# Seven half-size products of block sums in place of eight, on part of the FFN down projection of a hybrid encoder block

## The chip, the cores and the metric

The kernel runs on one core of one Trainium2 chip. The metric is the device time of one execution in microseconds (us), lower is better. TensorE (PE) does the matmuls, and its queue of weight loads is shown as PEld; VectorE (DVE), ScalarE (ACT) and GpSimd (POOL) do elementwise work; SyncE (SP) issues the DMAs of the weights.

## The reference, cut to what matters

The reference is one layer of an encoder block on 512 tokens of 1024 features: three token mixers, a gated merge, an output projection, and then a gated convolutional FFN with 2816 hidden features. Only the FFN matters here:

```python
def conv_glu_ffn(h, w_up, w_conv, b_conv, w_down):
    a, u = jnp.split(h @ w_up, 2, axis=-1)
    return (jax.nn.gelu(dwconv3(a, w_conv, b_conv)) * u) @ w_down

x = x + merged @ w_out[l]
x = x + conv_glu_ffn(rms_norm(x, ffn_norm_g[l]), w_ffn_up[l], w_ffn_conv[l], b_ffn_conv[l], w_ffn_down[l])
return rms_norm(x, final_norm_g)
```

Everything is float32. The down projection, the last product, has 2816 x 1024 weights and is applied to 512 tokens.

## The kernel before, in words

**Layout.** Activations lie transposed, features on the 128 partitions and the 512 tokens along the free axis, so that 1024 features are 8 tiles of 128 x 512 and the 2816 hidden features are 22 tiles. A matmul takes a 128 x 128 block of weights as the stationary operand and 512 tokens as the moving one, and adds into a PSUM tile of 128 x 512.

**Precision.** A float32 product is made of three matmuls in the fp32r format (`mm3`, L181 to L184): high part of the weights by high part of the activations, high by low, low by high. The high part is a copy rounded to fp32r on ACT, the low part a subtraction on DVE. Activations are split by `split_act` (L186 to L189) into the tiles named u; weights by `emit_split`, copy `wh` on ACT (L164) and subtraction `wl` on DVE (L165).

**Weights.** All weights lie in DRAM as one flat array of blocks in the order in which they are used (`block_list`, L51 to L79). A block is at most 1024 columns of 128 partitions, 512 KB, that is eight 128 x 128 blocks. `emit_raw` (L135 to L145) issues its DMA on SP (L144) into a ring of three raw buffers `wr`; `emit_split` splits it in one or two halves of up to 512 columns into rings of four `wh` and four `wl` buffers. `weights(key)` (L170 to L179) is called where a product begins: it issues the raw blocks up to three ahead and the splits up to one ahead of that product's block. So the DMA of a block stands in the program well before its use, and waits until the last reader of its raw buffer, a subtraction L165, is done.

**The order of the work.** The program is written as one sequence; a scheduler gives each engine its instructions and adds the semaphore waits. Each engine then runs its own queue strictly in order. Buffers come from rings (scratch tiles `s` of 512 columns, PSUM tiles `mm` and `at`, four each), and a ring's buffer is taken again once its last reader is done.

**The FFN** (L977 to L1032) runs twice, for `hh` = 0 and 1, each time over half of the hidden features, 11 tiles, in two stages.

- Up stage (L981 to L1010): for each of the 11 tiles two projections `ua` and `uu` of 24 matmuls of 512 columns each; on the first the convolution over tokens (`conv`, L308 to L317: DVE, ACT, DVE, DVE), gelu by Tanh (L1002 to L1005, ACT and DVE), a scaling on POOL (L1006); then the product with the second (L1009, DVE), and the split of the result into `UH[j]` and `UL[j]` (`split_act` at L1010).
- Down stage (L1011 to L1032): for each of the 8 feature tiles f, 11 contraction tiles of three matmuls of 512 columns into one PSUM tile (33 matmuls), then one DVE add into `x2[f]` (L1020). The weights of a feature tile are two blocks, of 8 and of 3 contraction tiles. In the second half each tile of x2 is squared on ACT (L1027 for f = 0, L1030), the square is added into `acc3` on POOL (L1031), and x2 is scaled on ACT (L1032). The last feature tile of the second half runs as two passes of 256 tokens, with the final norm and the stores (`finish_a`, `finish_b`, L917 to L975) between and behind them.

`_layout` (from L1040) builds the flat weight array on the host.

Of the kernel before, what the change touches and what calls it, by code (L numbers as in the profile page):

```python
# [50 lines left out]
def block_list():  # L51
# [20 lines left out]
    for hh in range(2):  # L72
        for f in range(HF * hh, HF * (hh + 1)):
            L.append((("ua", f), 1024))
            L.append((("uu", f), 1024))
        for f in range(8):
            for i, n in ((0, 8), (1, 3)):
                L.append((("dn", hh, f, i), n * 128))
    return L  # L79

# [8 lines left out]
BCOLS = {n: (lambda k: P) for n in ("mlk", "o", "xaq", "memk", "naq", "nak", "g", "out", "ua", "uu", "dn")}  # L89
# [6 lines left out]
def hybrid_block(ctx, tc, xT, memT, wflat, vecs, gbias, nabias, outa, outb):  # L96
# [34 lines left out]
    raws, split = {}, {}  # L131
    RAW_AHEAD, SPLIT_AHEAD = 3, 1
    st = {"raw": 0, "split": 0}

    def emit_raw(i):  # L135
        key, n = BLOCKS[i]
        _, off, _ = BINDEX[key]
        r = wp.tile([P, BW], F32, tag="raw", name=nm("wr"), bufs=3)
# [8 lines left out]
    def halves(i):  # L147
        n, c = BLOCKS[i][1], BCOLS[BLOCKS[i][0][0]](BLOCKS[i][0])
        k = n // c
        k0 = k if n <= HWD else (k + 1) // 2  # L150
        return c, [(0, k0)] + ([(k0, k)] if k0 < k else [])

    def emit_split(i):
        key, n = BLOCKS[i]
        r = raws.pop(i)
        c, hs = halves(i)
        split[i] = []
        for a, b in hs:
            h = wp.tile([P, HWD], F32R, tag="hi", name=nm("wh"), bufs=4)
            l = wp.tile([P, HWD], F32R, tag="lo", name=nm("wl"), bufs=4)  # L160
            m = (b - a) * c
            for u, v in ((0, P), (P, m)) if i == 0 and a == 0 else ((0, m),):
                src = r[:, a * c + u:a * c + v]
                A.activation(h[:, u:v], src, AF.Copy)  # L164
                V.tensor_tensor(l[:, u:v], src, h[:, u:v].bitcast(F32), op=ALU.subtract)  # L165
            for k in range(a, b):
                q = slice((k - a) * c, (k - a + 1) * c)
                split[i].append((h[:, q], l[:, q]))

    def weights(key):  # L170
# [37 lines left out]
    SY.dma_start(vec, vecs)  # L208
    emit_raw(0)
# [98 lines left out]
    def conv(ps, rbt, w, b, i, n):  # L308
# [4 lines left out]
        t1 = scr()  # L313
# [662 lines left out]

    for hh in range(2):  # L977
        gu = [unit(F32R) for _ in range(6)]
        UH = [gu[k // 4][:, (k % 4) * S:(k % 4 + 1) * S] for k in range(HF)]
        UL = [gu[3 + k // 4][:, (k % 4) * S:(k % 4 + 1) * S] for k in range(HF)]  # L980
        for j in range(HF):  # L981
# [18 lines left out]
            c = conv(pa, rb2, "ffw", "ffb", f, FT)  # L1000
# [9 lines left out]
            split_act(UH[j], UL[j], c, 0.5)  # L1010
        for f in range(KT):  # L1011
            ws = weights(("dn", hh, f, 0)) + weights(("dn", hh, f, 1))
            last = hh == 1 and f == KT - 1
            for a, b in ((0, 256), (256, 512)) if last else ((0, 512),):
                ps = mmps()[:, :b - a]
                for k in range(HF):
                    mm3(ps, ws[k][0], ws[k][1], UH[k][:, a:b], UL[k][:, a:b], k == 0, k == HF - 1)
                    if last and a > 0 and k == 7:
                        rb3 = row_a(dg3)
# [3 lines left out]
                elif last:  # L1023
                    finish_b(rb3)
# [111 lines left out]
```

## Time and profile before

| what | value |
|---|---|
| time, median of 3 executions | 921.71 us (920.74 to 921.77) |
| the profiled execution's own time | 921.14 us |
| its span, first to last instruction | 919.4 us |
| mean granted TensorE clock | 0.998 of full speed |
| DMA over the span | 96.39 MB, mean 105 GB/s |

The profile is of one execution on the one core. Each engine's busy time is also given as a share of the span. A row of the timeline has the start in us from the span's start, the duration in us, the engine, the line of the kernel, the operation, the tiles written and read with their shapes, and in square brackets how long the engine had been idle and which instruction released it. A row of a group has the shape, the count, the busy time in us and the mean duration of one in ns, and then the idle time before them with what ended most of it. Matmuls are pipelined: one of 512 columns is listed with some 390 ns although the next one starts earlier, so the pace of PE is read from the distance of starts, not from durations.

### The profile page before, as it was taken

To read this page: it belongs to the slowest core of one execution; us is meant where nothing else is said; L and a number is where in the kernel's file an instruction comes from. 1 tells how busy PE (TensorE), PEld (TensorE's weight loads), DVE (VectorE), ACT (ScalarE), POOL (GpSimd) and SP (SyncE) were. 2 spreads that over 40 slices of the span, in tenths; PEclk is the share of its full clock that TensorE was granted. 3 is DMA by queue.
4 is the path that set the end of the run, shared out by engine and by line. 5 is a ranking of instruction groups with operands and counts; after the bars stand their busy time and mean duration, and the time that the engine had idled before them with its cause. 6 is when DMAs were issued, how large, how long until landed. Compare 5 with 4: busy or idle time off the path is not lost.

```text
span 919.4 us, 12132 instructions
## 1 busy us (share of the span) xinstructions
PE 903.8 (98%) x4459; PEld 754.8 (82%) x4459; DVE 576.4 (63%) x979; ACT 437.1 (48%) x875; POOL 134.2 (15%) x155
## 2 busy tenths in 40 slices
PE   7999999999999999999999999999999999999996
PEld 5899888988888888788888887888888888888886
DVE  6893555746656668895445447777733477777333
ACT  7464445656445556564333434544422344444442
POOL 5000321112040301111121211111100011111112
PEclk9999999999999999999999999999999999999999
DMA  7223523422242323231223332322232322222222
GB/s 247 103 92 104 185 87 109 155 98 92 69 138 69 121 88 120 96 125 62 93 94 122 138 114 77 107 92 92 86 95 95 115 92 92 92 92 87 94 72 92
DMA packets 32939, 96.39 MB, mean 105 GB/s; under 512 B 4056, under 2 KB 7528, under 8 KB 32880
## 3 DMA queue, kind: packets, MB, share of 16 engines
q1 hardware_dynamic: 31440, 92.45, 29.7%
q0 software_dynamic: 1440, 3.17, 1.1%
q8 instruction: 35, 0.57, 0.3%
q14 instruction: 24, 0.20, 0.1%
HBM read 92.44 MB, written 3.16 MB: 104 GB/s over the span
## 4 chain that ended last, share of the span: by engine, by line
PE 96%; DVE 2%; issue 1%; DMA 0%; POOL 0%; ACT 0%; SPq 0%; POOLq 0%; DVEq 0%; ACTq 0%
PE mm L182 28%; PE mm L183 28%; PE mm L184 28%; PE at L529 2%; PE at L182 2%; PE at L183 2%; PE at L184 2%; PE at L665 1%; PE at L652 1%; DMA wr<-wflat 0%; POOL u L973 0%; PE at L742 0%; PE at L636 0%; PE at L637 0%; DVE s L884 0%
## 5 line engine op out<-in xcount | busy, mean ns | idle before, releaser
L182 PE MATMUL mm<-u,wh 128*128 128x512 f32 (+1 forms) x1115 | 436.6, 392 | 6.0 <-ACT wh L164 6.0
L184 PE MATMUL mm<-u,wl 128*128 128x512 f32 (+1 forms) x1115 | 433.3, 389 | 0.0
L183 PE MATMUL mm<-u,wh 128*128 128x512 f32 (+1 forms) x1115 | 433.1, 388 | 0.0
L164 ACT ACTIVATE wh<-wr 128x512 fp32r<-128x512 f32 (+3 forms) x305 | 189.5, 623 | 308.6 <-PE mm L183 274.1
L165 DVE TENSOR_TENSOR wl<-wr,wh 128x512 fp32r<-128x512 f32 (+3 forms) x305 | 236.3, 776 | 145.3 <-ACT wh L164 142.9
L182 PEld LDWEIGHTS mm<-u,wh 128*128 128x128 f32 x1115 | 210.1, 188 | 51.0 <-ACT wh L164 6.0
L184 PEld LDWEIGHTS mm<-u,wl 128*128 128x128 f32 x1115 | 210.0, 188 | 46.0
L183 PEld LDWEIGHTS mm<-u,wh 128*128 128x128 f32 x1115 | 210.1, 188 | 45.2 <-issue 0.5
L1006 POOL TENSOR_TENSOR s<-s,rb 128x512 f32<-128x512 f32 x22 | 29.1, 1325 | 267.2 <-DVE s L1005 255.2
L885 POOL TENSOR_TENSOR u<-u,s 128x512 f32<-128x512 f32 x16 | 22.4, 1399 | 166.2 <-DVE s L884 108.8
L188 ACT ACTIVATE u<-s 128x512 fp32r<-128x512 f32 x34 | 21.4, 629 | 52.4 <-DVE s L1009 50.8
L866 DVE TENSOR_TENSOR s<-mm,rb_x 128x512 f32<-128x512 f32 x24 | 16.6, 692 | 28.8 <-PE mm L184 28.8
L189 DVE SCALAR_TENSOR_TENSOR u<-s,u 128x512 fp32r<-128x512 f32 x34 | 23.5, 692 | 14.7 <-ACT u L188 14.4
L517 ACT ACTIVATE E<-R,bi 128x128 f32<-128x128 f32 x80 | 27.9, 394 | 1.8 <-POOL R L498 1.6
L314 ACT ACTIVATE s<-pad,vec 128x512 f32<-128x512 f32 x30 | 24.4, 813 | 8.6 <-DVE pad L312 8.6
L315 DVE SCALAR_TENSOR_TENSOR s<-pad,vec,s 128x512 f32<-128x512 f32 x30 | 22.5, 751 | 6.2 <-ACT s L314 6.2
L182 PE MATMUL mm<-wh,u 128*128 128x256 f32 (+1 forms) x80 | 24.5, 306 | 0.0
L183 PE MATMUL mm<-wl,u 128*128 128x256 f32 (+1 forms) x80 | 24.3, 304 | 0.0
L184 PE MATMUL mm<-wh,u 128*128 128x256 f32 (+1 forms) x80 | 24.3, 304 | 0.0
L1020 DVE TENSOR_TENSOR u<-mm,u 128x512 f32<-128x512 f32 (+1 forms) x17 | 11.2, 660 | 20.8 <-PE mm L184 20.8
L1005 DVE SCALAR_TENSOR_TENSOR s<-s,s 128x512 f32<-128x512 f32 x22 | 15.2, 692 | 13.4 <-ACT s L1004 13.3
L316 DVE SCALAR_TENSOR_TENSOR s<-pad,vec,s 128x512 f32<-128x512 f32 x30 | 22.5, 751 | 0.7
(223 smaller groups left out, 913.4 us busy)
## 6 DMA issues: line engine op xcount, KB each, us to landing
wr<-wflat SPq DMA_DIRECT2D x141, 512.0 KB, 3.3
s<-xT SPq DMA_DIRECT2D x16, 256.0 KB, 4.1
nab<-nabias SPq DMA_DIRECT2D x16, 256.0 KB, 2.6
wr<-wflat SPq DMA_DIRECT2D x17, 192.0 KB, 2.3
R<-rd SPq DMA_DIRECT2D x8, 256.0 KB, 3.5
u<-nav_d POOLq DMA_DIRECT2D x32, 64.0 KB, 2.9
wr<-wflat SPq DMA_DIRECT2D x2, 544.0 KB, 3.5
s<-memT SPq DMA_DIRECT2D x4, 256.0 KB, 3.7
```

The lines of the kernel that those rows point to most:

```text
L164: A.activation(h[:, u:v], src, AF.Copy)
L165: V.tensor_tensor(l[:, u:v], src, h[:, u:v].bitcast(F32), op=ALU.subtract)
L182: PE.matmul(ps, lh, rh, start=start, stop=False)
L183: PE.matmul(ps, lh, rl, start=False, stop=False)
L184: PE.matmul(ps, ll, rh, start=False, stop=stop)
L189: V.scalar_tensor_tensor(l, src, scale, h.bitcast(F32), op0=ALU.mult, op1=ALU.subtract)
L314: A.activation(t1, pad[:, 0:512], AF.Identity, scale=vcol(w, i), bias=vcol(b, i))
L315: V.scalar_tensor_tensor(t1, pad[:, 1:513], vcol(w, n + i), t1, op0=ALU.mult, op1=ALU.add)
L316: V.scalar_tensor_tensor(t1, pad[:, 2:514], vcol(w, 2 * n + i), t1, op0=ALU.mult, op1=ALU.add)
L517: A.activation(E[:, i, :], src, AF.Exp, bias=bi[:, d, abs(J - s), s, h:h + 1])
L885: G.tensor_tensor(mgv(f), mgv(f), tg[i], op=ALU.add)
L1006: G.tensor_tensor(c, c, rb2, op=ALU.mult)
```

## The change

The down projection is cut into pairs of feature tiles (f, f + 1 with f even) and, of the 11 contraction tiles of a half, into the first eight and the last three. For the first eight, the contraction is cut into two parts of four tiles (c tiles 0 to 3 and 4 to 7) and the tokens into two parts of 256. A pair is then a product of a 2 x 2 block matrix of weights (a11, a12 for feature tile f, a21, a22 for f + 1; each four blocks of 128 x 128) and a 2 x 2 block matrix of activations, eight half-size products. In seven of the eight pairs (all but f = 6 of the second half: `is_quad`) these are replaced by seven products of block sums, in the scheme that is known as Winograd's variant of Strassen's algorithm. Contraction tiles 8 to 10 are multiplied as before.

What is issued for it:

- **Weight sums**, per pair, in `form`: s1 = a21 + a22 and s3 = a11 - a21 on POOL (512 columns each), P6's factor = s1 - a11 and P3's factor = a12 - P6's factor on DVE (512 columns each). Every factor (P1, P4, P6, P5, P7, P2, P3) is split by an ACT copy and a DVE subtraction of 512 columns (`two`), and so are the two halves of the block for tiles 8 to 10 (384 columns each).
- **Activation sums**, in the up stage of each half, for j = 4 to 7, in `right_factors`: four DVE subtractions of 256 columns from the hidden tiles j - 4 and j, and two `split_act` of 512. Hidden tiles 0 to 3 are kept in float32 for it (`kept`). In the first half only the first 256 tokens of tiles 0 to 3 are split for direct use; the second half splits all 512, which its plain pair needs.
- **Products**, in `dn_quad`: 7 x 4 `mm3` of 256 columns, 3 `mm3` of 256 into each of P2's and P3's half for the first tile's contraction tiles 8 to 10, and 3 `mm3` of 512 for the second tile's. P1 and P6 share one PSUM tile, P5 and P7 one, P2 and P3 one.
- **Sums of the products**, on DVE into x2 directly, and U2 = P1 (copied by ACT) + P6 + P7 along the way.
- **Blocks**: the two blocks of 1024 columns of a pair come first, then one of 768 with tiles 8 to 10 of both features, in place of 1024, 384, 1024, 384.
- **Prefetch, everywhere in the kernel**: a block is no longer split as a whole one block ahead. The program holds a list of units (a half of a block, or one factor, in the order `FORMS`), and `weights` emits the units up to two behind the last one of the product that begins; a raw block is issued as soon as the program has let go of a ring buffer (`pump`). The rings keep their sizes (three raw, four `wh`, four `wl`).

```diff
+FORMS = ("P1", "P4", "P6", "P5", "P7", "P2", 0, "P3", 1)
...
-    RAW_AHEAD, SPLIT_AHEAD = 3, 1
+    RAW_BUFS, AHEAD = 3, 2
...
+    def form(m, i):
+        n = 4 * P
+        if m == "P1":
+            r0, r1 = raws[i[0]], raws[i[1]]
+            a11, a12, a21, a22 = r0[:, :n], r0[:, n:2 * n], r1[:, :n], r1[:, n:2 * n]
+            s1, s3 = scr(), scr()
+            G.tensor_tensor(s1, a21, a22, op=ALU.add)
+            G.tensor_tensor(s3, a11, a21, op=ALU.subtract)
+            quad.update(P1=a11, P2=a12, P5=s1, P7=s3, P4=a22)
+        elif m == "P6":
+            quad[m] = scr()
+            V.tensor_tensor(quad[m], quad["P5"], quad["P1"], op=ALU.subtract)
+        elif m == "P2":
+            quad["P3"] = scr()
+            V.tensor_tensor(quad["P3"], quad["P2"], quad["P6"], op=ALU.subtract)
+        h, l = two(quad[m], n)
+        return [(h[:, k * P:(k + 1) * P], l[:, k * P:(k + 1) * P]) for k in range(4)]
...
     def weights(key):
-        i, _, n = BINDEX[key]
-        while st["raw"] <= min(i + RAW_AHEAD, len(BLOCKS) - 1):
-            emit_raw(st["raw"])
-            st["raw"] += 1
-        while st["split"] <= min(i + SPLIT_AHEAD, len(BLOCKS) - 1):
-            emit_split(st["split"])
-            st["split"] += 1
-        return split.pop(i)
+        while st["unit"] <= min(last_unit[key] + AHEAD, len(units) - 1):
+            emit_unit(st["unit"])
+            st["unit"] += 1
...
+    def right_factors(ci, cj, hi, lo):
+        t = [scr(), scr()]
+        T1, T2, T3, T4 = t[0][:, :Hf], t[0][:, Hf:], t[1][:, :Hf], t[1][:, Hf:]
+        V.tensor_tensor(T1, ci[:, Hf:], ci[:, :Hf], op=ALU.subtract)
+        V.tensor_tensor(T2, cj[:, Hf:], T1, op=ALU.subtract)
+        V.tensor_tensor(T3, cj[:, Hf:], ci[:, Hf:], op=ALU.subtract)
+        V.tensor_tensor(T4, T2, cj[:, :Hf], op=ALU.subtract)
+        for n in range(2):
+            split_act(hi[:, n * S:(n + 1) * S], lo[:, n * S:(n + 1) * S], t[n], 0.5)
...
+    def dn_quad(hh, f, U, T):
...
+        ba, bb, bc, bd, ep = mmps(), atps(), atps(), atps(), mmps()
...
+        product("P1", ba[:, first], lambda e, i: U[e][i][:, first])
+        A.activation(U2, ba[:, first], AF.Copy)
+        add(X[:, 0], U2)
+        product("P4", bd[:, first], lambda e, i: T[e][i][3])
+        add(X[:, 2], bd[:, first], ALU.subtract)
+        product("P6", ba[:, second], lambda e, i: T[e][i][1])
+        add(U2, ba[:, second])
+        add(X[:, 1], U2)
+        product("P5", bb[:, first], lambda e, i: T[e][i][0])
+        add(X[:, 1:4:2], bb[:, first].unsqueeze(1).to_broadcast([P, 2, Hf]))
+        product("P7", bb[:, second], lambda e, i: T[e][i][2])
+        add(U2, bb[:, second])
+        add(X[:, 2:4], U2.unsqueeze(1).to_broadcast([P, 2, Hf]))
+        product("P2", bc[:, first], lambda e, i: U[e][4 + i][:, first], False)
+        ws = weights((("dp", hh, f), 0))
+        plain(bc[:, first], first)
+        add(X[:, 0], bc[:, first])
+        product("P3", bc[:, second], lambda e, i: U[e][4 + i][:, second], False)
+        plain(bc[:, second], second)
+        add(X[:, 1], bc[:, second])
+        ws = weights((("dp", hh, f), 1))
+        for i in range(3):
+            mm3(ep, *ws[i], U[0][8 + i], U[1][8 + i], i == 0, i == 2)
+        add(x2[f + 1], ep)
...
+        for f in range(0, KT, 2):
+            if is_quad(("dn", hh, f)):
+                dn_quad(hh, f, U, T)
+                if hh == 1:
+                    squares(f)
+                    squares(f + 1)
+            else:
+                dn_plain(hh, f, U)
+                squares(f)
+                dn_plain(hh, f + 1, U)
```

`squares` is the three passes L1027 to L1032, moved into a function and run for both tiles behind a pair; `dn_plain` is the down stage of before for the last two tiles; `pump`, which `weights` calls through `emit_unit`, issues the DMA of the next block whenever fewer than three are held. Eight or nine buffers of activations (`up_tiles`) take the place of six.

More of the change, by code (lines that the diff above doesn't have):

```diff
@@ L145, in emit_raw @@
         raws[i] = r
[L147 to L168, printed above, removed]
@@ L208, in hybrid_block @@
     SY.dma_start(vec, vecs)
+    list_units()
     emit_raw(0)
@@ L977, in hybrid_block @@
     for hh in range(2):
[L978 to L980 removed]
+        U, T, both = up_tiles(hh == 1)
+        kept = []
         for j in range(HF):
```

167 lines of the change are left out of this document (131 added, 36 removed).

## The prediction

> **What bounds the kernel now.** I read the page's totals and its chain of work first, then the timeline of the down projection.
>
> ```profile
> span 919.4 us, 12132 instructions
> PE 903.8 (98%) x4459; PEld 754.8 (82%) x4459; DVE 576.4 (63%) x979; ACT 437.1 (48%) x875; POOL 134.2 (15%) x155
> PE 96%; DVE 2%; issue 1%; DMA 0%; POOL 0%; ACT 0%; SPq 0%; POOLq 0%; DVEq 0%; ACTq 0%
> ```
>
> The reader is to see that TensorE carries 96% of the chain: work taken from PE comes off the time, as long as nothing else becomes late. The next rows are the down projection's pace (first and last of eight adds, one per feature tile) and that stage's busy time.
>
> ```profile
> 671.14 0.69 DVE L1020 TENSOR_TENSOR u<-mm,u 128x512 f32<-128x512 f32 x1 [1.15 <-PE mm L184]
> ...
> 724.65 0.69 DVE L1020 TENSOR_TENSOR u<-mm,u 128x512 f32<-128x512 f32 x1 [0.97 <-PE mm L184]
> ```
> ```profile
> core 0: us, PE busy (x) PEld busy (x) DVE busy (x) ACT busy (x) POOL busy (x), PEclk, DMA share, GB/s
> ...
> 602.20:613.30 11.10, 11.10 (x50) 9.01 (x49) 8.47 (x11) 5.04 (x8) 1.29 (x1) 1.00 0.27 97
> 675.00:695.00 20.00, 20.00 (x88) 16.19 (x87) 6.65 (x12) 4.74 (x8) 0.00 (x0) 1.00 0.31 96
> ```
>
> Seven tiles take 53.51 us: 7.644 us a tile, and at 33 matmuls of 512 columns 0.2316 us each. PE never pauses and its clock is whole; DVE works a third of the stage (6.65 of 20 us). That idle third engine is what the change spends.
>
> **What is removed from PE.** One tile, the last, already runs as half-size products:
>
> ```profile
> 899.89 0.28 PE L182 MATMUL mm<-u,wh 128*128 128x256 f32 x1
> ...
> 903.62 0.28 PE L184 MATMUL mm<-u,wl 128*128 128x256 f32 x1
> ```
>
> These are the first and last of 33 matmuls: 3.73 us over 32 intervals, 0.1166 us each, 0.6% more than half of 0.2316. A changed pair of tiles issues 7 products x 4 contraction tiles x 3 = 84 matmuls of 256 columns, 18 more of 256 for contraction tiles 8 to 10 of the first tile, and 9 of 512 for the second: 102 x 0.1166 + 9 x 0.2316 = 13.98 us, against 2 x 7.644 = 15.29. That is 1.31 us a pair, **9.2 us for the seven pairs**, the most the change can give here.
>
> **What is added on DVE.** Prices:
>
> ```profile
> 568.90 0.69 DVE L165 TENSOR_TENSOR wl<-wr,wh 128x512 fp32r<-128x512 f32 x1
> 569.50 0.69 DVE L1005 SCALAR_TENSOR_TENSOR s<-s,s 128x512 f32<-128x512 f32 x1
> 570.10 0.69 DVE L312 TENSOR_TENSOR pad<-mm,rb 128x512 f32<-128x512 f32 x1
> ```
> ```profile
> L165 DVE TENSOR_TENSOR wl<-wr,wh 128x384 fp32r<-128x384 f32 x17 | 9.5, 558 | 26.5 <-ACT wh L164 26.4
> L1020 DVE TENSOR_TENSOR u<-mm,u 128x256 f32<-128x256 f32 x2 | 0.8, 417 | 3.1 <-PE mm L184 3.1
> ```
>
> An operation of 512 columns starts every 0.60 us; I take 0.47 for 384 and 0.34 for 256 (their durations less the same 0.09 of overlap). A pair now has 7 low parts of 512, 2 of 384, two block sums of 512 (P6, P3), three adds of 512 and seven of 256: 12 x 0.60 + 2 x 0.47 + 7 x 0.34 = 10.5 us in 14.0 us of PE. By sums it fits. ACT (seven copies of 512, two of 384, one of 256, in the second half four passes over x2) stays near 8 us. In the up projection four of eleven tiles of each half get four subtractions of 256 and two splits of 512 more, 2.6 us of DVE beside the 8.47 us busy in an 11.1 us tile (602.20 row). I cost this at nothing: two weight blocks of lookahead hide it; with that cover gone it would be up to 1 us for each of eight tiles.
>
> **POOL and the port.** A pair's two sums s1 (for P5, P6) and s3 (P7) go to POOL:
>
> ```profile
> 736.20 1.29 POOL L1006 TENSOR_TENSOR s<-s,rb 128x512 f32<-128x512 f32 x1 [71.03 <-DVE s L1005]
> 736.24 1.79 DVE L165 TENSOR_TENSOR wl<-wr,wh 128x512 fp32r<-128x512 f32 x1
> ```
> ```profile
> 347.53 0.68 DVE L638 TENSOR_TENSOR s<-at,nab 128x512 f32<-128x512 f32 x1
> 347.69 1.29 POOL L885 TENSOR_TENSOR u<-u,s 128x512 f32<-128x512 f32 x1 [1.70 <-DVE s L884]
> 348.13 1.40 DVE L165 TENSOR_TENSOR wl<-wr,wh 128x512 fp32r<-128x512 f32 x1
> ```
>
> A DVE operation on two SBUF operands that starts under a POOL add ends 0.54 us after it (738.03 against 737.49; 349.53 against 348.98): it waits the add out. One that reads PSUM (L638) keeps its 0.68. The Trainium skill, page "SBUF — State Buffer" (the part on the shared port pair), says that DVE with two SBUF inputs and a GpSimd operation exclude each other for the whole instruction, the loser blocking fully; the trace agrees. This rule speaks against the change: low parts and block sums are such operations.
>
> **The path.** Built, the changed kernel's PE order in a pair is P1, P4, P6, P5, P2, P7, tiles 8 to 10 into P2's half, three or four matmuls of the second tile's product, P3, the rest. P3 shares a PSUM buffer with P2, so it waits for DVE's add of P2's half; that add stands in DVE's queue behind others. In the second and third pair of the first half the queue before it holds the next pair's P6 sum (which needs s1), the 512 add of U2 and the last low part. And s1 needs the next pair's second block, whose buffer P2's low part frees. Its legs:
>
> ```profile
> 673.73 0.63 ACT L164 ACTIVATE wh<-wr 128x512 fp32r<-128x512 f32 x1 [2.14 <-PE mm L183]
> ...
> 674.39 0.69 DVE L165 TENSOR_TENSOR wl<-wr,wh 128x512 fp32r<-128x512 f32 x1 [1.96 <-ACT wh L164]
> ```
> ```profile
> 512.46 0.69 DVE L165 TENSOR_TENSOR wl<-wr,wh 128x512 fp32r<-128x512 f32 x1
> ...
> 513.17 0.33 SPq L144 DMA_DIRECT2D wr<-wflat  x1
> 513.21 0.61 ACT L910 ACTIVATE s<-u 128x512 f32<-128x512 f32 x1
> ...
> 513.97 1.29 POOL L911 TENSOR_TENSOR acc<-acc,s 128x512 f32<-128x512 f32 x1 [4.28 <-ACT s L910]
> ```
> ```profile
> DMA to landing us min/median/max: 2.3/3.2/4.2
> ```
>
> From P4's end on PE: ACT copy 0.66, DVE backlog 0.2 (my estimate) and low part 0.69, so 1.55; SP issues 0.02 later (513.15 to 513.17) and the block lands 3.2 later, 4.77; POOL starts some 0.1 after its releaser (513.82 to 513.97), s1 1.29, 6.16; s3 follows at once and holds the port 1.29 more, 7.45; P6 sum 0.60, U2 add 0.60, low part 0.59: **9.24 us**. PE reaches the matmul that needs that low part after 57 x 0.1166 + 2 x 0.2316 + 2 x 0.1166 = 7.34. It stands still for 1.9 us, twice: **3.8 us**. Without the hold it would be 0.6 each.
>
> In the first pair of each half and the second of the second half the P6 sum stands later; there s1 starts within 0.2 us of the U2 add that it would hold up (both about 6.3 us after P4's end). Where POOL is first, P3 starts 0.8 to 1.0 us late. That is nothing or 2.8 us; nearest to a coin, **1.4**.
>
> In the second half the passes over x2 stand on ACT ahead of the next pair's P6 copy:
>
> ```profile
> 670.71 0.39 PE L184 MATMUL mm<-u,wl 128*128 128x512 f32 x1
> ```
> ```profile
> 862.71 0.63 ACT L1030 ACTIVATE s<-u 128x512 f32<-128x512 f32 x1 [0.33 <-DVE u L1020]
> 863.38 0.72 ACT L1032 ACTIVATE u<-u,vec 128x512 f32<-128x512 f32 x1
> 863.49 1.30 POOL L1031 TENSOR_TENSOR acc<-acc,s 128x512 f32<-128x512 f32 x1 [15.06 <-ACT s L1030]
> ```
> ```profile
> 738.67 0.63 ACT L188 ACTIVATE u<-s 128x512 fp32r<-128x512 f32 x1 [2.46 <-DVE s L1009]
> ...
> 739.20 0.62 ACT L164 ACTIVATE wh<-wr 128x512 fp32r<-128x512 f32 x1
> ```
> ```profile
> L948 ACT ACTIVATE s<-at 128x256 f32<-128x256 f32 x1 | 0.4, 384 | 2.8 <-PE at L946 2.8
> ```
>
> From the pair's last matmul's start: DVE's add starts 0.43 later (670.71 to 671.14), ends at 1.12; Square 0.67 (862.71 to 863.38), scaling 0.62 (its 0.72 less 0.1 of overlap), P6's copy 0.55 (one after another start 0.53 apart, 738.67 to 739.20), copy of U2 0.4 (the 384 ns row): 3.4 us, against 0.23 + 24 x 0.1166 = 3.03 on PE. With the copy for P5 behind it I take 0.65 us before the second pair and 0.65 before the third, where POOL's add into acc (1.30) also holds one block sum: 1.1 more. **2.4 us**.
>
> Elsewhere the instructions before the first changed pair stand in the same order on PE; one x load stands behind one more weight block on SP at the start: 0 to 0.7 us, I take **0.3**. The fourth pair has no successor and loses 0.1.
>
> Weight DMAs: the same bytes in 21 blocks for 28 on these pairs, stage share 0.31; no cost. Buffers: P7 after P5 waits for one DVE add, covered by P2 between them.
>
> **Sum.** -9.2 + 3.8 + 1.4 + 2.4 + 0.3 + 0.1 = -1.2 us. The profiled execution ran 921.14 us (span 919.4 and 1.7 around it): **919.9 us**. That execution is 0.57 under the median shown, 921.71, so against the median it is -1.8 us, the very edge of 0.2% (about what a measurement of this kernel tells from no change).
>
> **Rivals.**
> 1. The hold is not paid: DVE gets its P6 sum in before s3, or slack swallows it. Then the second and third pairs lose 0.6 each, ties nothing, the acc hold nothing: -9.2 + 1.2 + 1.3 + 0.4 = -6.3, **914.8 us**. For: DVE has 3 us of slack a pair. Against: s3 waits for nothing new when s1 ends, and each L165 under an L1006 add took 1.79. Chance 0.2.
> 2. Slower: POOL does both sums in a row wherever DVE waits, in every pair that has a successor, so the port is away 2.6 us and not 1.3 where I counted a tie: three pairs lose 2.1 to 2.3 in place of a half of 0.9, +5.3: **925.2 us**. It decides as soon as the mean wait passes 1.31 us a pair. For: s1 and s3 are neighbours in POOL's queue and have the same block to wait for. Against: in the quoted rows a waiting DVE goes next. Chance 0.24. It is the full price of the exclusive lock that the Trainium skill tells of (page "SBUF — State Buffer", the part on the shared port pair).
> 3. The half-size products are no halves: each matmul brings a weight load of 188 ns,
>
> ```profile
> L182 PEld LDWEIGHTS mm<-u,wh 128*128 128x128 f32 x1115 | 210.1, 188 | 51.0 <-ACT wh L164 6.0
> ```
>
> and if that paced them, 714 x 0.071 = +51 us, 971 us. Against: 33 of them ran at 0.1166 in this trace. Chance 0.02.
>
> **How the numbers follow.** The forecast has 0.54: it reaches from 917.3 (no ties lost, the two long waits 0.5 shorter) to 922.5 (all ties lost, 0.7 at the start, waits 0.3 longer). The range 914.6 to 925.4 takes in rivals 1 and 2, and leaves out the rest. Faster by over 0.2% (under 919.87): rival 1 and four tenths of the forecast, 0.42. Within: most of the rest of it, 0.32. Slower (over 923.55): rivals 2 and 3, 0.26.
>
> **What would show it.** Right: matmuls of 256 columns 0.117 us apart; in the second and third changed pair of the first half a PE pause near 1.9 us ended by DVE's low part, behind a P6 sum that ends after s3; pauses before P6 in the second half ended by ACT. Wrong: DVE operations under s1 and s3 at 0.69 (rival 1); pauses over 2 us before P3 in first pairs (rival 2); pauses in the up projection, or blocks that land later than 3.6 us, would break the sum outside it.

## The result and the profile after

The changed kernel takes 937.07 us in the median of 4 executions (935.09 to 938.55), the kernel before 921.57 us in the median of 4: a ratio of 1.0169 with a 95% interval of 1.0156 to 1.0182. The forecast was 919.9, and its range ended at 925.4. The profiled execution ran 935.09 us with a span of 933.4, so 14.0 us above the span of before.

The page of the changed kernel, its totals:

```profile
span 933.4 us, 12988 instructions
PE 904.4 (97%) x4774; PEld 768.2 (82%) x4774; DVE 629.4 (67%) x1118; ACT 455.2 (49%) x919; POOL 162.1 (17%) x169
```

There are 315 more matmuls, as counted: 45 for each of seven pairs. Busy time of PE did not fall; a part of the reason, matmuls at half pace, is shown further down. The next view has idle time of PE: its waits over the whole span (what it waited for, us in total, times, longest us), cut to those that matter here:

```profile
PE mm L251 <- DVE wl L202: 5.4, 3, 2.3
PE at L251 <- DVE wl L202: 3.4, 2, 1.7
PE mm L249 <- ACT s L1106: 2.3, 3, 1.1
PE at L249 <- DVE u L1103: 1.4, 2, 0.7
...
PE at L319 <- POOL acc_x L352: 0.6, 1, 0.6
```

None of these five rows has a counterpart in the kernel before. Four are in the down projection: low parts (L202), the copy U2 (L1106) and adds (L1103) come late. The fifth is at the very start.

Now the down projection pair by pair. The rows are the first matmuls of the first two pairs of the first half:

```profile
664.40 0.28 PE L249 MATMUL mm<-u,wh 128*128 128x256 f32 x1
...
683.26 0.28 PE L249 MATMUL mm<-u,wh 128*128 128x256 f32 x1
```

The first pair takes 18.86 us where 13.98 were worked out. This table has the times of the pairs, each from such a row to the next (where a pause ends a pair, the next pair's first two matmuls stand ahead of the pause in PE's order, and the edge between the two can be some 0.1 off). The runs are explained below.

| kernel | 1st half: 1st, 2nd, 3rd pair | 2nd half: 1st, 2nd pair | median us |
|---|---|---|---|
| changed | 18.86, 18.66, 17.86 | 18.80, 15.06 | 937.07 |
| no activation sums | 16.31, 16.66, 16.37 | 16.33, 16.00 | 928.35 |
| new deal of tiles | 16.42, 14.20, 14.15 | 16.30, 14.89 | 921.86 |
| sums on DVE | 19.62, 15.56, 14.30 | 18.24, 15.70 | 931.47 |
| P3's tile alone | 17.93, 14.78, 14.29 | 19.16, 15.04 | 926.84 |
| P6's tile alone | 17.69, 18.37, 16.54 | 20.13, 14.90 | 936.50 |
| new deal, no activation sums | 14.24, 14.28, 14.29 | 14.13, 14.91 | 918.29 |
| scaling on DVE, old tiles | 15.53, 16.87, 17.91 | 15.58, 16.39 | 927.83 |
| new deal, scaling on DVE | 14.11, 14.19, 14.15 | 14.11, 14.89 | 915.75 |

**The first pair.** The timeline of PE, ACT and DVE there:

```profile
666.48 0.63 ACT L1172 ACTIVATE s<-s 128x512 f32<-128x512 f32 x1
...
668.06 0.36 ACT L1106 ACTIVATE s<-mm 128x256 f32<-128x256 f32 x1
...
668.47 0.39 PE L249 MATMUL mm<-u,wh 128*128 128x256 f32 x1 [1.07 <-ACT s L1106]
...
669.62 0.69 DVE L1177 TENSOR_TENSOR s<-mm,s 128x512 f32<-128x512 f32 x1 [1.18 <-POOL s L1174]
...
673.03 0.69 DVE L202 TENSOR_TENSOR wl<-wr,wh 128x512 fp32r<-128x512 f32 x1
...
673.77 0.39 PE L251 MATMUL at<-u,wl 128*128 128x256 f32 x1 [1.72 <-DVE wl L202]
```

PE ended the up projection at 664.40. The Tanh of the last up tile (L1172) runs on ACT 2 us later, the product of that tile (L1177) on DVE 5 us later; the copy U2 and P2's low part stand behind them in the queues. P6 writes the second half of the PSUM tile whose first half U2's copy reads, and so waits for the copy.

How DVE came to be that late is seen from the up projection's last products with `uu`, first in the kernel before and then in the changed one:

```profile
610.20 0.68 DVE L1009 TENSOR_TENSOR s<-mm,s 128x512 f32<-128x512 f32 x1
621.29 0.68 DVE L1009 TENSOR_TENSOR s<-mm,s 128x512 f32<-128x512 f32 x1
...
665.63 0.68 DVE L1009 TENSOR_TENSOR s<-mm,s 128x512 f32<-128x512 f32 x1
```
```profile
612.33 0.69 DVE L1177 TENSOR_TENSOR s<-mm,s 128x512 f32<-128x512 f32 x1 [1.18 <-POOL s L1174]
624.30 0.69 DVE L1177 TENSOR_TENSOR s<-mm,s 128x512 f32<-128x512 f32 x1 [1.18 <-POOL s L1174]
```

A tile with activation sums takes DVE 11.97 us, not 11.09, while PE goes on at its own pace. The busy times of the engines in that tile (PE, PEld, DVE, ACT, POOL, then the granted clock, DMA share and GB/s) tell why:

```profile
612.33:624.30 11.97, 11.97 (x53) 9.76 (x52) 9.73 (x17) 5.96 (x10) 1.67 (x1) 1.00 0.26 89
```

DVE is busy for 9.73 us only. The other 2.2 us are nearly all waits in the gelu's own chain, in which DVE hands over to another engine and needs the answer before it can go on: 1.18 for POOL's scaling (L1174), 0.70 for ACT's Tanh (L1172) and 0.29 for ACT in the convolution.

At the last tile DVE is at 669.62, against 665.63 before: 3.99 us later, of which PE's own lateness is only 1.10 (its first matmul of the stage is at 664.40, and before at 670.71 - 32 x 0.2316 = 663.30). DVE is **2.9 us behind** when the down projection begins.

**The second and third pair** of the first half pause where the prediction had them. The second pair's rows:

```profile
687.76 0.33 SPq L186 DMA_DIRECT2D wr<-wflat  x1
...
691.87 1.29 POOL L212 TENSOR_TENSOR s<-wr 128x512 f32<-128x512 f32 x1 [11.84 <-DMA wr<-wflat]
693.11 1.28 POOL L213 TENSOR_TENSOR s<-wr,wr 128x512 f32<-128x512 f32 x1
693.19 1.74 DVE L217 TENSOR_TENSOR s<-s,wr 128x512 f32<-128x512 f32 x1 [1.19 <-POOL s L212]
...
694.86 0.68 DVE L1103 TENSOR_TENSOR u<-u,s 128x512 f32<-128x512 f32 x1
695.46 0.55 DVE L202 TENSOR_TENSOR wl<-wr,wh 128x384 fp32r<-128x384 f32 x1
...
696.06 0.50 PE L251 MATMUL mm<-u,wl 128*128 128x512 f32 x1 [2.26 <-DVE wl L202]
```

The chain is the forecast one, link by link: block, s1, s3 holding the port while the P6 sum waits (1.74 us for 0.69), U2's add, low part. Only the landing took 4.0 us and not 3.2 (POOL starts 4.11 after the issue, 0.1 of it its own); in the third pair it took 3.6. But this pair is 4.7 us too long, and the pause is only 2.3 of it. Most of the rest is in the windows, whose column behind POOL is the granted clock:

```profile
core 0: us, PE busy (x) PEld busy (x) DVE busy (x) ACT busy (x) POOL busy (x), PEclk, DMA share, GB/s
...
696.00:698.00 2.00, 1.94 (x11) 1.85 (x12) 0.94 (x3) 0.00 (x0) 0.00 (x0) 0.82 0.47 144
698.00:700.00 2.00, 2.00 (x12) 2.00 (x11) 0.64 (x1) 0.63 (x1) 0.00 (x0) 0.50 0.13 52
700.00:702.00 2.00, 2.00 (x11) 1.78 (x11) 1.17 (x3) 0.81 (x2) 0.00 (x0) 0.82 0.39 68
714.00:716.00 2.00, 1.97 (x8) 1.84 (x9) 0.91 (x2) 0.00 (x0) 0.00 (x0) 0.59 0.44 138
716.00:718.00 2.00, 2.00 (x12) 2.00 (x11) 0.00 (x0) 0.63 (x1) 0.00 (x0) 0.56 0.15 58
```
```profile
697.10 0.29 PE L250 MATMUL at<-u,wh 128*128 128x256 f32 x1
...
697.60 0.42 PE L250 MATMUL at<-u,wh 128*128 128x256 f32 x1
697.81 0.42 PE L251 MATMUL at<-u,wl 128*128 128x256 f32 x1
```

Behind each of these two pauses TensorE runs at half clock: matmuls of 256 columns start 0.21 us apart and not 0.117. The lost clock sums to 2 x (0.18 + 0.50 + 0.18) = 1.72 us behind the first pause and 2 x (0.41 + 0.44) = 1.70 behind the second. The kernel before has no such stretch in this stage.

### The profile page after: what moved, and what is told of

The parts are those of the page before. It is cut to its first block, busy times and chain, and to the rows that moved or that the text cites. A ratio compares the mean times of both kernels' runs of the same rounds, so it can differ in the third digit from the quotient of the medians.

```text
span 933.4 us, 12988 instructions
## 1 busy us (share of the span) xinstructions
PE 904.4 (97%) x4774; PEld 768.2 (82%) x4774; DVE 629.4 (67%) x1118; ACT 455.2 (49%) x919; POOL 162.1 (17%) x169
## 5 line engine op out<-in xcount | busy, mean ns | idle before, releaser
L249 PE MATMUL mm<-u,wh 128*128 128x512 f32 (+1 forms) x1024 | 396.9, 388 | 8.8 <-ACT wh L201 6.5
L251 PE MATMUL mm<-u,wl 128*128 128x512 f32 (+1 forms) x1024 | 392.9, 384 | 5.4 <-DVE wl L202 5.4
L250 PE MATMUL mm<-u,wh 128*128 128x512 f32 (+1 forms) x1024 | 392.7, 384 | 0.0
L202 DVE TENSOR_TENSOR wl<-wr,wh 128x512 fp32r<-128x512 f32 (+3 forms) x298 | 215.6, 725 | 99.6 <-ACT wh L201 98.6
L249 PEld LDWEIGHTS mm<-u,wh 128*128 128x128 f32 x1024 | 193.1, 189 | 48.5 <-ACT wh L201 6.7
L251 PEld LDWEIGHTS mm<-u,wl 128*128 128x128 f32 x1024 | 193.1, 189 | 46.0 <-DVE wl L202 6.0
L250 PEld LDWEIGHTS mm<-u,wh 128*128 128x128 f32 x1024 | 193.4, 189 | 38.9 <-issue 0.5
L251 PE MATMUL at<-u,wl 128*128 128x256 f32 x182 | 52.2, 289 | 3.4 <-DVE wl L202 3.4
L249 PE MATMUL at<-u,wh 128*128 128x256 f32 x182 | 53.8, 296 | 1.4 <-DVE u L1103 1.4
L250 PE MATMUL at<-u,wh 128*128 128x256 f32 x182 | 52.5, 288 | 0.0
L1174 POOL TENSOR_TENSOR s<-s,rb 128x512 f32<-128x512 f32 x14 | 23.5, 1678 | 132.3 <-DVE s L1173 123.4
L249 PEld LDWEIGHTS at<-u,wh 128*128 128x128 f32 x182 | 35.6, 196 | 4.5 <-DVE u L1103 3.2
L251 PEld LDWEIGHTS at<-u,wl 128*128 128x128 f32 x182 | 35.5, 196 | 4.0 <-DVE wl L202 4.0
L250 PEld LDWEIGHTS at<-u,wh 128*128 128x128 f32 x182 | 35.7, 196 | 0.1
L1174 POOL TENSOR_TENSOR c<-c,rb 128x512 f32<-128x512 f32 x8 | 12.9, 1620 | 91.6 <-DVE c L1173 91.6
```

Source lines behind the costliest of these rows:

```text
L202: V.tensor_tensor(l[:, u:v], src[:, u:v], h[:, u:v].bitcast(F32), op=ALU.subtract)
L249: PE.matmul(ps, lh, rh, start=start, stop=False)
L250: PE.matmul(ps, lh, rl, start=False, stop=False)
L251: PE.matmul(ps, ll, rh, start=False, stop=stop)
L1174: G.tensor_tensor(c, c, rb2, op=ALU.mult)
```

## The experiments

Three theories. **Lag**: the activation sums make DVE late, and the first pair of each half pays. **Tiles**: the products wait because they share PSUM tiles with a product just before them, whose result is still being read, and because the order on PE was made around that. **Hold**: the long pauses (of the second and third pair of the first half) are the late sums on POOL and their hold of the port. Each run is set against executions of the kernel before that were timed beside it (medians 921.02 to 921.28); ratios and intervals are to these, and "less" without more is against the changed kernel's 937.07.

**1. The prefetch alone.**

```diff
 def is_quad(key):
-    return key[0] == "dn" and key[2] % 2 == 0 and (key[1], key[2]) != (1, 6)
+    return False
```

(with `dn_plain` for all pairs, and no activation sums)

> All pairs run as plain products (no block sums, no activation sums, the matmuls of the kernel before), but with the new list of units, the new prefetch distance and the DMAs issued as soon as a buffer is let go. Theory: the changed kernel's TensorE runs 1.10 us later than before from the gates of the first mixer on, because the later x tiles stand behind one more weight block on SP; then this kernel takes 921.6 + 1.1 = 922.7 us. Rival: the 1.1 us belong to one execution or to something else; then 921.6 within 0.3. If the prefetch is what costs in the down projection too, over 925.

922.79 us against 921.13 for the kernel before, ratio 1.0023 (1.0014 to 1.0032). The theory's 922.7 is met. The down projection has no pause; the loss is at the start, in the waits of PE:

```profile
PE at L319 <- POOL acc_x L352: 2.5, 1, 2.5
```

**2. No activation sums.**

```diff
-            elif j < 8:
-                right_factors(kept[j - 4], c, both[0][j - 4], both[1][j - 4])
...
-            T.append([[q(i // 2, 4 * (i % 2) + t, Hf) for t in range(4)] for i in range(4)])
+            T.append([[U[e][4 + i][:, t % 2 * Hf:(t % 2 + 1) * Hf] for t in range(4)] for i in range(4)])
```

> The sums of the activations (four subtractions of 256 columns and two splits of 512 in each of four up tiles a half) are left out; the products P4 to P7 read split hidden tiles 4 to 7 in their place, so the numbers that come out are other ones. Everything else is as in the changed kernel. Theory (lag): those sums put DVE 2.9 us behind TensorE by the end of the up projection, and the first pair of each half pays for it (18.86 and 18.80 us in place of 13.98); without them the first pairs take 14.0 to 15.0 and the kernel 937 - 8 = 929 us, 928 to 931. Rival (banks): the first pairs lose their time because P6 writes the PSUM tile whose other half ACT still copies, and P3 the tile whose other half DVE still adds; then at least 3 us a pair stay, 934 or more. The long pauses in the second and third pair of the first half stay in either case.

928.35 us (1.0082, 1.0059 to 1.0106), 8.7 us less than the changed kernel. The first pairs fall by 2.5 us each, less than forecast: they keep a pause before P2's low part and one before P3 (0.66 and 0.73 us in the first half). The second and third pairs lose their stretches at half clock in this execution, though pauses of 1.7 us stay. So the time that was forecast came about in part by another way. The execution shown is the fastest of four (927.02, mean granted clock 0.997); the slowest, 931.60, had 0.993, so it very likely had such stretches.

**3. New deal of PSUM tiles.**

```diff
-        product("P6", ba[:, second], lambda e, i: T[e][i][1])
+        product("P6", bb[:, first], lambda e, i: T[e][i][1])
...
-        product("P5", bb[:, first], lambda e, i: T[e][i][0])
+        product("P5", ba[:, second], lambda e, i: T[e][i][0])
...
-        product("P7", bb[:, second], lambda e, i: T[e][i][2])
+        product("P7", bd[:, second], lambda e, i: T[e][i][2])
...
-        product("P3", bc[:, second], lambda e, i: U[e][4 + i][:, second], False)
+        product("P3", bb[:, second], lambda e, i: U[e][4 + i][:, second], False)
```

(and the adds that read them)

> Only the PSUM tiles of the products are dealt otherwise: P6 goes to the tile of P3, P5 to that of P1, P7 to that of P4, so that no product writes a tile whose other half was written by the product just before it or the one before that. Theory (lag): the waits before P6 and P3 (1.07, 0.65, 1.04, 0.72, 0.17 us) go, but the low parts for P2 come no earlier, so the pauses before P6 move to them; the kernel gains 1 to 2 us, 935 to 936. Rival (banks): these waits, with the refill of 0.1 to 0.2 behind each, were the loss; 4.4 us gained or more, 932.5 or less.

921.86 us (1.0006, 0.9996 to 1.0015): 15.2 us less, so the theory failed, and the gain is far beyond the 4.4 us that the rival counted. My count had left out that the tiles also decide the order. Built, P7 now stands ahead of P2, and P3 ahead of all matmuls of the second feature tile. Of the waits in the down projection's first half, one is left, before P7 in the first pair; the second half has its twin and two of 0.28 us behind ACT's copies:

```profile
PE mm L249 <- ACT wh L201: 7.0, 3, 6.5
PE at L249 <- DVE u L1103: 4.0, 2, 2.0
```

(6.5 us of the first row are the start of the kernel.)

**4. The weight sums on DVE.**

```diff
-            G.tensor_tensor(s1, a21, a22, op=ALU.add)
-            G.tensor_tensor(s3, a11, a21, op=ALU.subtract)
+            V.tensor_tensor(s1, a21, a22, op=ALU.add)
+            V.tensor_tensor(s3, a11, a21, op=ALU.subtract)
```

> The two weight sums s1 and s3 of a pair run on DVE in place of POOL (0.6 us each there, no hold of the port). Theory (hold): in the second and third pair of the first half s1, the hold by s3 and the P6 sum no longer stand ahead of the last low part; from P4's end 1.55 + 4.0 (the landing as traced) + 0.1 + 0.6 + 0.6 = 6.9 us against 7.34 on TensorE, so the pauses of 2.3 and 2.1 us go, and with them the two stretches of 3.4 us at half clock (1.7 us each): 8 us gained, 929 us, 927 to 931. Rival (load): DVE is the bound, 1.2 us more of it in a pair cost what the hold cost, and the pauses stay: 935 or more.

931.47 us (1.0114, 1.0091 to 1.0137), 5.6 us less, not the 8 that were expected. The hold is real: the pauses of the second and third pair go from 2.26 and 1.94 us to 0.55 and 0.20 in one pair and none in the other. The first pairs don't gain (19.62 and 18.24), with 2.05 us before P2's low part in each, since DVE has yet more to do there.

**5 and 6. The two parts of the new deal.** Run 5 moves P3 alone, into the second half of P4's tile:

```diff
-        product("P3", bc[:, second], lambda e, i: U[e][4 + i][:, second], False)
+        product("P3", bd[:, second], lambda e, i: U[e][4 + i][:, second], False)
```

> Of the new deal of PSUM tiles only one part: P3 goes to the second half of P4's tile in place of the second half of P2's. P6 still shares P1's tile and P7 P5's. Built, TensorE's order then has P3 ahead of all nine matmuls of the second feature tile, where the changed kernel has three or four of them ahead of P3. Theory (order through the tile): because P3 shares P2's tile, the scheduler filled the wait with matmuls that need the pair's last low part, the one behind the held P6 sum; with P3 first it is needed 21 x 0.1166 = 2.45 us later. The pauses of 2.3 and 2.1 us, the two stretches at half clock (1.7 us each) and the waits before P3 (0.65, 0.72) go: 9 us gained, 928 us, 926 to 930. Rival (hold): the chain through POOL is too late wherever its consumer stands; less than 4 us gained, 933 or more.

926.84 us (1.0060, 1.0045 to 1.0075), 10.2 us less. POOL does what it did, and yet the long pauses are gone; the two pairs take 14.78 and 14.29 us. What remains of the waits is nearly all in the first pairs:

```profile
PE at L251 <- DVE wl L202: 3.4, 2, 1.7
PE mm L249 <- ACT s L1106: 2.6, 4, 1.1
```

Run 6 moves P6 to the first half of a tile of its own and P5 to the second half of P1's, and leaves P3:

> The other part: P6 in the first half of a tile of its own (P7 follows in its second half) and P5 in the second half of P1's; P3 stays in P2's tile, with the matmuls of the second feature tile ahead of it. Theory: the waits before P6 (1.07, 1.04, 0.17 us and the refill behind each) go, and little else, since the long pauses in the second and third pair have another cause: 2 to 4 us gained, 933 to 935. Rival: if the late DVE alone sets the first pairs, under 1 us gained, 936 or more; if the sharing of P1's tile is most of what the new deal gained, over 8 us, 929 or less.

936.50 us (1.0166, 1.0148 to 1.0184): nothing that could be told from the changed kernel, where 2 to 4 us were expected. In the profiled execution the five pairs are 1.6 us shorter than in the changed kernel's, but 3.6 us more had gone before the first of them, behind a wait of 1.84 us at the start and 6.83 us at half clock. The waits before P6 went, and came back before P7 and P3:

```profile
PE at L249 <- DVE s L1103: 5.8, 2, 3.0
PE at L249 <- DVE u L1103: 5.6, 3, 2.5
```

P7 waits for U2's add, which reads P6 from the same tile, and DVE is late with it. So of the deal, P3's place is the larger part. The other 5 us came when P6, P5 and P7 moved with it (run 3); that P6's place is worth something only where P7 is moved as well follows from these waits, and was not run alone.

**7. New deal, no activation sums** (the edits of 2 and 3).

> The new deal of tiles and, with it, the sums of the activations left out (products P4 to P7 read split hidden tiles 4 to 7 in their place, the numbers that come out are other ones). Under the new deal one pause of 2.16 and one of 2.11 us are left, before P7 in the first pair of each half, ended by a DVE add. Theory (lag): these are DVE's 2.9 us of lag from the sums; without the sums they go, 921.9 - 4.3 = 917.6 us, 916.5 to 918.7. Rival (the pair's own chain): they stay at 1 us or more each, 920 or more. Against the kernel without the sums under the old deal (928.4) the new deal is then worth 11 us, not 15.

918.29 us (0.9972, 0.9960 to 0.9985). The first pairs take 14.24 and 14.13 us, with no wait in them: the pauses that the new deal had left were the lag. The executions of this run spread from 916.37 to 919.88, with mean granted clocks from 0.997 down to 0.994, so stretches at half clock are likely a part of that; the one profile is of the fastest, and has none before its last microseconds.

**8. New deal, and the gelu scaling on DVE.**

```diff
-            G.tensor_tensor(c, c, rb2, op=ALU.mult)
+            V.tensor_tensor(c, c, rb2, op=ALU.mult)
```

> The new deal of tiles and, in the up projection, the scaling of the gelu's result by the row factor on DVE in place of POOL. DVE idles 1.18 us in each up tile until POOL has done it; on DVE it takes 0.60. Theory (lag): DVE's period in the four tiles with activation sums falls from 11.97 to 11.4 us and the lag at the end from 2.9 to 1 or less, so that the pauses of 2.16 and 2.11 us before P7 shrink under 1 us: 921.9 - 2.5 = 919.4 us, 918 to 920.5. Rival (load): an operation more on the busy engine, in 18 tiles that had no need of it, costs what it saves; 921.5 or more.

915.75 us (0.9944, 0.9929 to 0.9959): faster than the kernel before, and by more than expected. In the two profiles 4.5 of the 7.35 us between run 3 and this one are the two first pairs; the other 2.8 lie at the start, where run 3's execution waited 1.56 us for acc_x and ran 3.41 us at half clock and this one did neither, and that can't be put down to the scaling. For the first pairs, the groups of DVE between 600 and 665 us show the reason, in the changed kernel and then here (shapes, count, busy us, mean ns, idle before):

```profile
L1177 DVE TENSOR_TENSOR s<-mm,s 128x512 f32<-128x512 f32 x6 | 4.2, 692 | 7.1 <-POOL s L1174 7.1
```
```profile
L1174 DVE TENSOR_TENSOR s<-s,rb 128x512 f32<-128x512 f32 x5 | 4.4, 883 | 0.1
L1177 DVE TENSOR_TENSOR s<-mm,s 128x512 f32<-128x512 f32 x6 | 4.1, 689 | 0.2
```

Waits of 1.18 us for POOL, one in each tile, became operations of 0.88 us on DVE (the window cuts off one of six). All three pairs of the first half and the first of the second now take 14.11 to 14.19 us.

**9 and 10. Towards a best version.** Run 9 adds to run 8 the x tiles' place at the start:

```diff
-        while st["raw"] < len(BLOCKS) and (st["raw"] <= i or len(raws) < RAW_BUFS):
+        while st["raw"] < len(BLOCKS) and (st["raw"] <= i or len(raws) < RAW_BUFS and st["raw"] <= st["cap"]):
...
     def weights(key):
+        b = BINDEX.get(key, (9,))[0]
+        st["cap"] = b + 3 if b < 4 else len(BLOCKS)
```

> The new deal of tiles, the gelu scaling on DVE, and the weight DMAs at the very start held back as before the change, so that SP issues the x tiles in the order of before. Theory: the changed kernel and all runs of the new prefetch lose about 1.1 us at the start (0.6 to 1.8 of it seen as TensorE waiting for POOL's sum of the squares of x), which goes: 915.7 - 1.1 = 914.6 us. Rival: the wait there varies from execution to execution whatever the order on SP, 915.4 or more.

914.23 us (0.9929, 0.9915 to 0.9944). The wait for acc_x is not among PE's waits any more. But neither was it in the profile of run 8, and the intervals of the two overlap, so the 1.5 us between them are not settled.

Run 10 adds the later squares, as its expectation tells (a pair's tiles are put on the list `late` in place of being squared right behind it):

```diff
+        for g in late:
+            squares(g)
+        late.clear()
         product("P5", ba[:, second], lambda e, i: T[e][i][0])
```

> As the run with the x order, and in the second half the squares and scalings of a pair's two x2 tiles are written behind the next pair's sixth product's wait, ahead of its P5, in place of right behind the pair. Theory: the passes stood on ACT ahead of the next pair's copies (pauses of 0.44, 0.44 and 0.18 us before P5 and behind); later they stand behind them: 914.6 - 1.0 = 913.6 us. Rival: they meet the copies of P5 and P7 there instead and the pauses move: 914.4 or more.

913.83 us (0.9923, 0.9907 to 0.9940), the fastest of all. PE waits for nothing from the first up tile to the final norm; the second pair of the second half takes 14.36 us, 0.53 less than in run 9. The medians differ by 0.4 us, which four executions of each can't tell from none.

**11 and 12. Two controls of the scaling.** It alone in the kernel before:

> The kernel before with only the gelu scaling on DVE in place of POOL. Theory: there DVE was never late, TensorE runs through the up projection without a pause, and nothing changes: 921.3 us within 0.5. Rival: the move is a gain of its own, without block sums, and the 6 us that the new deal and it gained together over the new deal alone belong to it: 919 or less.

921.53 us (1.0005, 0.9995 to 1.0014): worth nothing there. And it alone in the changed kernel, under the old deal of tiles:

> The changed kernel with only the gelu scaling on DVE, under the old deal of tiles. Theory (lag): the first pairs lose what they lose without the activation sums, not more, as the lag is gone: 928.4 us as there, 926.5 to 930.5; the pauses of 2.3 and 2.1 us in the second and third pair stay. Rival: the lag needs more than 0.6 us a tile to go, 933 or more.

927.83 us (1.0077, 1.0062 to 1.0092), 9.2 us less. The first pairs fall from 18.86 and 18.80 to 15.53 and 15.58, and the long pauses stay (1.96 and 1.88 us). Its wait for acc_x at the start was 1.48 us.

## Why the prediction was wrong

**PE's saving was right.** With the waits out of the way a pair takes 14.1 to 14.4 us, against 13.98 worked out and 15.29 before. Rival 3 is refuted; weight loads don't pace the products.

**The step that failed** is this one: "I cost this at nothing: two weight blocks of lookahead hide it; with that cover gone it would be up to 1 us for each of eight tiles." Each of the eight tiles does cost DVE 0.74 to 0.88 us. The count behind it, 2.6 us of sums beside 8.47 of busy time in 11.1, took all idle time for room. But 2.2 us a tile went by in waits of the gelu's chain, with the sums there to be done, so they lengthened DVE's tile. The lookahead does hide that from PE inside the up projection, which has no pause in any run. But it covers PE only. The tiles without sums gave DVE 0.5 us of 3.4 back, and it entered the down projection 2.9 us late, where every product needs a fresh low part and a PSUM half read out. The price was 18.86 + 18.80 for two pairs where 2 x (13.98 + 0.47) stood in the sum: 8.8 us too little. The lag is the larger part of that: without it these two pairs take 5.0 us less (run 2) and 6.6 us less (run 12). What then stays of their excess, 4.7 and 3.2 us, goes with the new deal of tiles, and the lag's share under the new deal is 4.4 us (16.42 and 16.30 in run 3, 14.24 and 14.13 in run 7). By the medians its removal is worth 8.7 and 9.2 us under the old deal, with half-clock stretches that came and went in it.

**The second failure is a term that was not there.** The pauses of the second and third pair were priced at 1.9 us each and measured 2.43 and 2.10 by the distance of starts (693.51 to 696.06, and its twin, less one matmul's 0.117). That mechanism was right, and the landing was the mis-sized link (4.0 and 3.6 us for 3.2). The 3.4 us lost at half clock behind them were in no sum.

**The start** was taken at 0.3 us and cost 1.10 in the profile. The mechanism was the named one: the x load that SP issued at 8.66 us before now stands behind one more weight block and goes out at 13.81. The run with the prefetch alone put 1.7 us between its median and that of before.

**The ties** were lost in the first pairs. In the first of them POOL's s1 starts 0.3 us ahead of U2's add, and P3 waits:

```profile
677.05 1.29 POOL L212 TENSOR_TENSOR s<-wr 128x512 f32<-128x512 f32 x1 [7.46 <-DMA wr<-wflat]
677.35 1.54 DVE L1103 TENSOR_TENSOR u<-u,s 128x512 f32<-128x512 f32 x1
678.30 1.73 POOL L213 TENSOR_TENSOR s<-wr,wr 128x512 f32<-128x512 f32 x1
...
679.28 0.38 PE L249 MATMUL at<-u,wh 128*128 128x256 f32 x1 [0.65 <-DVE u L1103]
```

By the distance of starts P3 is 0.80 us late there and 0.88 in the second half, where 0.8 to 1.0 was written; without the lag the wait stays (0.73 us in run 2, 0.66 in run 12), and with the sums on DVE (run 4) it is gone from both first pairs. The second half's second pair lost no such tie. That pair and the third lost some 3.4 us in the profile, where 2.4 + 0.47 stood: about right in sum, but the waits for ACT were 0.17 and 0.23 us and not 0.65, and a wait of 1.20 us in the third pair, behind two block sums that POOL's adds into acc held (1.64 and 1.66 us for 0.69), was the largest single one.

The terms close: the profile is 15.2 us above the sum. 8.8 are the first pairs, 4.8 the second and third pair of the first half (3.4 of it clock), 0.8 the start, 0.8 all the rest. The changed kernel's median is 2.0 us above that execution, its fastest; the others' lower mean clocks (0.990 to 0.992, where it had 0.994) make more half-clock stretches the likely reason. (One slip of adding: the forecast's own band, 917.3 to 922.5, comes to 917.5 and 922.3 by the terms beside it. Nothing hangs on it.)

**What lay beneath was in the prediction, and not drawn out.** It said that P3 waits for DVE's add of P2's half, and that three or four matmuls of the second feature tile stand ahead of P3. It then asked only when their low part comes. Run 5 asks why they stand there: with P3 in another tile the order changes, the low part is needed 21 matmuls later, and 10.2 us go, without one instruction less on POOL. The page "PSUM — Partial Sum Buffer" of the Trainium skill (section "PSUM bank collisions raise a hardware error") says that accesses of two engines must be kept apart by bank and quadrant of 32 partitions, or more simply by bank, and not by address: one to other columns of the same bank collides too. The trace agrees in so far as products were made to wait for reads of the other half of their tile (P6 for U2's copy, 1.07 us). These waits are set by the program; what an unguarded access would do was not tried.

**Rival 2** gave the right sign by a wrong mechanism: in the rows above U2's add runs between s1 and s3, so POOL does not do both in a row, and no first pair has the pause of over 2 us before P3 that it called for. POOL held the port, but the larger part of the loss came through DVE's lag and the shared tiles. **Rival 1** falls with the same rows: the hold is paid. Taking POOL's sums away (run 4) brought 5.6 of the 15.5 us back. The gains of the runs are not shares that can be added up: no activation sums (8.7) and the new deal (15.2) would be 23.9 us, and together they gave 18.8 (run 7). One removal also shortens pauses, and takes away half-clock stretches, that the other would have taken.

## What to carry to other kernels

When an edit adds work to an engine that "has room", don't ask only whether the bounding engine is covered in that stage: take the waits in its own chain out of that room, work out how late the loaded engine leaves the stage, and who needs it in the first microseconds of the next. Deal PSUM tiles so that no product writes a tile whose other half was filled just before, and read the built order with an eye on what stands there only to fill such a wait. The block sums do pay here, 7.2 us of the 9.2 that PE can give (913.83 against 921.02), once the lag and the tiles are seen to.

## What the runs showed of the hardware

**Short pauses can halve the clock, by where they fall.** A pause is counted here from the distance of two starts, less one matmul's normal distance. In these traces a pause of PE in the down projection of 1.87 to 3.11 us (18 of them in the changed kernel and runs 2 to 6 and 12) was followed by a stretch of 3.41 us at 0.50 in 7 cases, so by a loss of 1.7 us; no shorter pause there was. It is not the length alone: 1.87 us was enough once (run 5), and 3.11 us once was not (run 6). The traces show what decides. In every one of them the granted clock changes only at whole multiples of 3.413 us, counted from its first rise to full speed; in the changed kernel at 11.21, 697.29, 700.71, 714.36, 717.77 and 929.40 us, which is 0, 201, 202, 206, 207 and 269 steps. Three such steps around the first long pause (the step with the pause, the one behind it, the next):

```profile
693.88:697.29 3.41, 1.23 (x8) 1.15 (x9) 3.06 (x5) 0.00 (x0) 0.51 (x1) 1.00 0.08 22
697.29:700.70 3.41, 3.41 (x18) 3.41 (x18) 0.69 (x1) 0.72 (x2) 0.00 (x0) 0.50 0.27 94
700.71:704.12 3.41, 3.41 (x26) 3.19 (x25) 3.08 (x6) 2.08 (x4) 0.00 (x0) 1.00 0.51 154
```

With the pauses laid on these steps, the six that took 2.05 us or more out of a single step all had half clock in the next step. Of the two that took 1.87 and 1.89 us the first had it. None of the ten that took 1.65 us or less out of any one step had it, among them the pause of 3.11 us, which fell with 1.47 and 1.65 us on two steps. So the limit in these traces lies between 1.65 and 2.05 us of idle time in one step, about half of it, and whether a pause of some 2 us costs 1.7 us more is a matter of where it falls. (Pauses at the start of the kernel, among matmuls of other shapes, are not counted; behind waits there half clock came in runs 3 and 6.) The page "TensorE: Matmul & The Clock Gate" of the Trainium skill (section "The HAM clock gate") tells of a free-running window of 3413 ns, and of half rate after an idle one. The step of 3.413 us agrees with that window. But no pause here emptied a whole one, and the advice of that page of the Trainium skill (section "Why this matters for your kernels"), no idle gaps above some 3 us between bursts, is too lax for these traces. An estimate from the 1.7 us: the spread of the changed kernel's executions, 3.5 us, is that of two such stretches, and their mean clocks (0.994 in the fastest, 0.990 to 0.992 in the others) go with it.

**The port works both ways.** In the up projection POOL's scaling took longer when a low part was running as it began:

```profile
656.53 0.68 DVE L202 TENSOR_TENSOR wl<-wr,wh 128x512 fp32r<-128x512 f32 x1
656.74 1.62 POOL L1174 TENSOR_TENSOR s<-s,rb 128x512 f32<-128x512 f32 x1 [8.67 <-DVE s L1173]
```

1.62 us, where the same scaling took 1.29 in the kernel before when it began ahead of the low part: read so, it waited for DVE, as DVE waits for POOL elsewhere.
